# Hybrid attention trunk on one core: eight weight copies spread ahead of the attention, the product with the values' differences two projection steps later, eight projection steps behind the attention

## The chip, the cores and the metric

The kernel runs on one core of a Trainium2 chip. A time is the device time of one execution in microseconds (us). The kernel before took 801.21 us (median of three runs, 800.34 to 802.48). A difference of 0.3%, 2.4 us, is about what a measurement of this kernel can tell from no change.

## What is computed

One layer over 512 tokens of width 2048, all in float32: RMS norm, a sliding-window attention with 32 query heads on 4 key/value heads (window 128, a bucketed relative bias, a sink per head), a gate, an output projection, and then a gated embedding with a second 2048 x 2048 product. Cut to what matters here (the other mixers of the reference are not used at depth 1):

```python
hn = rmsnorm(x, norm_g[0])
q, k, v, gate = split(hn @ w_in)
probs = softmax_with_sink(q @ k.T * 64 ** -0.5 + bias, window 128)
x = x + ((probs @ v) * silu(gate)) @ w_out
emb = p @ ple_proj
x = x + emb * sigmoid(rmsnorm(x, ple_norm) @ ple_gate)
return rmsnorm(x, final_g)
```

## The kernel before

**Arithmetic.** TensorE multiplies numbers that are split into a high and a low part. `mm3` (L123 to L128) issues three matmuls for each product: high by high, low by high, high by low. A weight tile of 128 x 1024 arrives by DMA from SyncE's queue (`wraw`, L102), ScalarE casts the high part (`whi`, L109), VectorE subtracts to get the low part (`wlo`, L110). `wraw`, `whi` and `wlo` have three buffers each.

**Stages.** In the first stage (to about 71 us) the keys, values and first two query tiles are projected. Then thirty further tiles, 14 of q and 16 of the gate (`qps`, `gps`), are projected in 480 steps (16 for a tile, three matmuls each) by the generator `projections`. The first 40 steps (`AHEAD`) run by themselves. The other 440 are dealt out over the attention: the loop over `i` (L906) has 64 blocks of 32 queries and three more turns, and each turn issues the parts of several blocks in a fixed order with six or seven projection steps between them. That order is written out by hand for all engines, so each engine does its instructions as the program issued them.

**A turn of the attention.** Parts of it are generators, and each `next` issues the piece up to the following `yield`. `scores(i)` gives the scores (`s`, L478), bias and minimum on VectorE, the exponential on ScalarE (L522), the reciprocal, and the scaled weights (`pr`, L535). `turn(i - 2)` transposes on TensorE (`pt`, L546), casts on ScalarE (`r`, L557), subtracts on VectorE (L558), then lets GpSimd cut out the triangle (`own`, L565) and ScalarE copy it to the other half (`own`, L574). `weigh(j)` works on a pair of blocks, every second turn: a product of `r` with the values (`o`, L586) and, for the later blocks, a product of `own` with the difference of two value blocks (`o`, L588). A copy on ScalarE (`tmp`, L597) and an addition on VectorE (`u`, L599) then empty the bank. `r` and `own` have one buffer each. The differences are made in the first turns (`make_diff`, L379) and sent to `DV` by SyncE (`spread_diff`, L440).

**Chores.** When a projected tile is done, its three follow-ups go on the list `chores`. For q these are a scaling (L325), a cast (L336) and a subtraction (L334), for the gate L629, L630 and L623. Once the values of a head group are in `u`, `gate_value` (L613) goes on the list `idle`.

**Weight sums.** The output products later use sums of weight blocks. `sum_weights(i)` makes them in DRAM: for even `i` a copy of 512 KB from DRAM to DRAM on SyncE's queue (L692), for odd `i` a DMA of GpSimd that adds another block to a copy made seven steps before (L694). The eight first copies (`SUMS_EARLY` is 16) are issued together, at the end of turn 0.

**After the attention** the remaining chores run, and `unit` multiplies the gated values by `w_out` (`o<-bhi,fho`); its weights are loaded as `braw` (L723) and split as `bhi` and `blo` (L730, L731). In this stage VectorE also makes sums and splits of the gated values (`gate`, `flo`, L835 to L848).

Of the kernel before, what the change touches and what calls it, by code (L numbers as in the profile page):

```python
# [21 lines left out]
KC = D // P  # L22
# [33 lines left out]
def trunk_kernel(ctx: ExitStack, tc: tile.TileContext, a: dict):  # L56
# [25 lines left out]
    def bank(name, tag):  # L82
        return others.get(tag, psum).tile([P, 512], F32, tag=tag, name=name)
# [99 lines left out]
    kinds = [(kind, next(number[kind])) for kind in order]  # L183
# [173 lines left out]
    def make_key(h):  # L357

        t, e = divmod(h, 2)
        k = K[h] = kvq.tile([P, S // QB, 2, QB], F32R, tag="k", name=f"k{h}", bufs=2)  # L360
        same = slice(64 * e, 64 * e + 64)

        def part(low):
            src = kt[t][same].rearrange("p (j k) -> p j k", k=QB)
            for o in (slice(0, 64), slice(64, 128)):
                if low:
                    nc.vector.tensor_sub(k[o, :, 1], src, k[same, :, 0].bitcast(F32))
                else:
                    nc.scalar.copy(k[o, :, 0], src)

        return partial_of(part, False), partial_of(part, True)
# [31 lines left out]
    for b in range(exact, BUCKETS):  # L403
        d = np.nonzero(bk == b)[0]
        if len(d):
            lo, n = P - 1 + int(d.min()), len(d)
# [35 lines left out]
    def first_chores(i, step):  # L442

        if step == 0 and i < NB - 1:
            make_diff(i + 1)
        if step and 1 <= i < NB:
            diffs[i][step - 1]()
        if step == 2 and 1 <= i - 1 < NB:
            spread_diff(i - 1)
        if step and 1 <= i - 2 < NB:  # L450
            split(V[i - 2], values[i - 2])[step - 1]()
# [87 lines left out]
    def turn(i):  # L539


        d, g = divmod(i, UNITS)
        pr = T.pop(i)
        pt = bank(f"pt{i}", "t")[:, :256]
        for u in range(2):
            nc.tensor.transpose(pt[:, u * P : (u + 1) * P], pr[:, u, :], ident)  # L546

        j, part = divmod(i, 2)
        if part == 0:
            own = None  # L550
            if g >= P // TQ:
                own = apool.tile([P, 2, S], F32R, tag="own", name=f"own{j}")
            PT[j] = apool.tile([P, 2, S], F32R, tag="r", name=f"r{j}"), own
        r, own = PT[j]
        rh, rl = (r[:, l].rearrange("p (h t u q) -> p t u h q", h=GROUP, t=2, u=2)[:, part] for l in range(2))
        src = pt.rearrange("p (u h q) -> p u h q", u=2, h=GROUP)
        nc.scalar.copy(rh, src)  # L557
        nc.vector.tensor_sub(rl, src, rh.bitcast(F32))  # L558
        yield
        b = j % 2  # L560
        flat = lambda v, rows: v[rows].rearrange("p l (h t q) -> p t (l h) q", h=GROUP, t=2)[:, part]
        if own is not None:
            rows = slice(0, P) if b else slice(0, HB)
            sign = -1 if b else 1
            nc.gpsimd.affine_select(  # L565
                out=flat(own, rows), in_=flat(r, rows).bitcast(F32), pattern=[[0, 2 * GROUP], [sign, TQ]],
                compare_op=ALU.is_ge, fill=0.0, base=(-HB - 1 if b else 0) + sign * part * TQ, channel_multiplier=-sign,
            )
        yield
        if own is not None:  # L570
            here, there = slice(HB, P), slice(0, HB)
            if not b:
                here, there = there, here
            nc.scalar.copy(flat(own, there)[:, :GROUP], flat(own, here)[:, GROUP:].bitcast(F32))  # L574

    def weigh(j):

        kv, m = divmod(j, S // HB)
        n, b = divmod(m, 2)
        r, own = PT.pop(j)  # L580
        if m == 0:
            U[kv] = apool.tile([P, 4, S], F32, tag="u", name=f"u{kv}", bufs=2)
        out = bank(f"o{j}", "o")
        first = V[0 if n == 0 else n - 1 + b][:, kv]
        for low in range(2):
            nc.tensor.matmul(out, first, r[:, low], start=low == 0, stop=own is None and low == 1)  # L586
        if own is not None:
            nc.tensor.matmul(  # L588
                out, DV[:, n - 1, b, kv * 2 * HD : (kv + 1) * 2 * HD], own[:, 0], start=False, stop=True
            )  # L590
        yield
        ops = out.rearrange("p (u e q) -> p u e q", u=4, e=2)
        dst = U[kv][:, :, m * HB : (m + 1) * HB]
        lower, upper = slice(0, 64), slice(64, 128)
        tmp = [apool.tile([P, 4, HB], F32, tag=f"tmp{e}", name=f"tmp{e}_{j}") for e in range(2)]
        for e, (o, x) in enumerate(((lower, upper), (upper, lower))):
            nc.scalar.copy(tmp[e][o], ops[x, :, e, :])  # L597
        for e, o in enumerate((lower, upper)):
            nc.vector.tensor_add(dst[o], ops[o, :, e, :], tmp[e][o])  # L599
        if m == S // HB - 1:  # L600
            for c in range(4 * kv, 4 * kv + 4):
                weighed.add(c)
                if c in open_gates:
                    idle.append(partial_of(gate_value, c))
# [3 lines left out]
    chores, idle = [], []  # L608
# [78 lines left out]
    SUMS_EARLY = 16  # L687

    def sum_weights(i):

        if i % 2 == 0 and i // 2 < len(copies):
            nc.sync.dma_start(*copies[i // 2])  # L692
        elif i % 2 == 1 and 0 <= i // 2 - 3 < len(adds):
            nc.gpsimd.dma_start(*adds[i // 2 - 3], accum_op=ALU.add, max_dma_last_dim=8192)  # L694
# [181 lines left out]
    def some(of, n=1):  # L876
        for _ in range(min(n, len(of))):
            of.pop(0)()
# [5 lines left out]
    AHEAD = 5 * KC // 2  # L884
    for n in range(AHEAD):
        next(proj)
        if n % 4 == 3 and W.todo:
            W.todo.pop(0)()
        if n > KC and n % 2:
            some(chores)  # L890
    blocks = KVH * UNITS

    def sums_in(i):


        if i == 0:
            return range(0, SUMS_EARLY, 2)
        if i < 4:
            return range(4 * i + 3, min(4 * i + 7, SUMS_EARLY), 2)
        n, of = SUM_STEPS - SUMS_EARLY, blocks - 4  # L900
        return range(SUMS_EARLY + (i - 4) * n // of, SUMS_EARLY + (i - 3) * n // of)

    left = KC * len(kinds) - AHEAD

    softmax = iter(())
    for i in range(blocks + 3):  # L906

        before, softmax = softmax, scores(i) if i < blocks else iter(())
        turned = turn(i - 2) if 2 <= i < blocks + 2 else iter(())
        value = weigh(i // 2 - 2) if 4 <= i and i % 2 == 0 else iter(())  # L910
        next(value, None)
        next(turned, None)
        next(softmax, None)
        next(turned, None)
        next(before, None)
        next(softmax, None)
        first_chores(i, 0)
        if i in (6, 20, 36):
            idle.extend(make_key(1 + i // 16))
        todo = left // (blocks + 2 - i) if i < blocks + 2 else 0  # L920
        left -= todo
        for n in range(max(todo, 6)):
            if n < todo:
                next(proj)
            if n == 0:
                first_chores(i, 1)
                some(W.todo)
                some(chores or idle)
            elif n == 2:
                next(value, None)  # L930
                if len(chores) > 1:
                    some(chores)
            elif n == 3:
                next(turned, None)
                next(softmax, None)
            elif n == 4:
                first_chores(i, 2)
                some(chores or idle)
            elif n == 5:
                next(softmax, None)  # L940
        if i < blocks:
            for n in sums_in(i):
                sum_weights(n)
    for _ in proj:
        pass
    while chores or idle:
        some(chores or idle)
    during.close()
# [429 lines left out]
    n = done[3]  # L1378
# [87 lines left out]
```

## Time and profile before

| what | us |
|---|---|
| median of three runs | 801.21 |
| the profiled execution's own time | 801.74 |
| its span, first to last instruction | 800.0 |
| TensorE busy | 784.2 |
| VectorE busy | 583.8 |
| ScalarE busy | 517.9 |
| GpSimd busy | 150.6 |
| idle time of TensorE that ends on another engine | 6.4 |

The last row adds four lines of the view of waits: 5.0, 0.6, 0.5 and 0.3 us. The profiled execution took 1.74 us more than its span and 0.53 us more than the median. A matmul's duration in the trace is longer than the distance between two starts, since matmuls are pipelined; a busy share of TensorE near 100% therefore says that there is no gap, and the number of matmuls in a stretch says how fast they went. The column PEclk is the share of TensorE's full clock that was granted, the DMA column the busy share of the 16 DMA engines.

### The profile page before, as it was taken

What the parts mean: (1) busy time and instruction counts of PE and PEld (TensorE: products, weight loads), DVE (VectorE), ACT (ScalarE), POOL (GpSimd) and SP (SyncE); (2) the same over time, 40 slices, a digit from 0 to 9 for tenths busy, and PEclk for the clock granted to TensorE, in tenths of its full rate; (3) what the DMA queues carried; (4) which work ended last, traced back from release to release, by engine and by line L of the source; (5) the groups of instructions that cost most, each with busy time, mean ns of one, the idle gap of its engine ahead of it and who ended that gap; (6) DMA issues with size and microseconds to landing.
All of it is one profiled execution on the core that took longest, in us unless ns stands there. A gap on an engine that the chain in (4) does not pass through costs nothing.

```text
span 800.0 us, 11168 instructions
## 1 busy us (share of the span) xinstructions
PE 784.2 (98%) x3658; PEld 650.4 (81%) x3658; DVE 583.8 (73%) x1171; ACT 517.9 (65%) x1131; POOL 150.6 (19%) x252
## 2 busy tenths in 40 slices
PE   9999997999999999999999999999999999999995
PEld 8888885888888888888888887888888888888885
DVE  4538556876876768766776899778877666888896
ACT  6634356877777667766666754457689656756765
POOL 0031121343233413333234200000000020210000
PEclk9999998999999999999999999999999999999998
DMA  9782699999998997989797698767873996796633
GB/s 349 227 245 94 210 241 309 271 261 272 267 262 215 257 257 190 284 209 303 192 267 166 158 353 299 241 207 226 277 264 123 344 197 204 161 232 203 194 105 106
DMA packets 44618, 184.87 MB, mean 231 GB/s; under 512 B 6720, under 2 KB 7232, under 8 KB 39440
## 3 DMA queue, kind: packets, MB, share of 16 engines
q1 hardware_dynamic: 36480, 142.94, 52.0%
q0 software_dynamic: 8080, 41.22, 27.3%
q8 instruction: 29, 0.48, 0.2%
q14 instruction: 29, 0.24, 0.1%
HBM read 177.26 MB, written 62.97 MB: 300 GB/s over the span
## 4 chain that ended last, share of the span: by engine, by line
PE 89%; DVE 3%; DMA 3%; ACT 2%; issue 2%; POOL 0%; SPq 0%; ACTq 0%; DVEq 0%; POOLq 0%
PE gps L126 7%; PE gps L127 7%; PE gps L128 7%; PE qps L126 6%; PE qps L127 6%; PE qps L128 6%; PE g L126 5%; PE g L127 5%; PE g L128 5%; PE o L127 4%; PE o L128 4%; PE o L126 4%; DMA wraw<-in_w_gate_in 2%; PE s L478 2%; PE vps L286 2%; PE o L586 2%
## 5 line engine op out<-in xcount | busy, mean ns | idle before, releaser
L730 ACT CAST bhi<-braw 128x1024 fp32r<-128x1024 f32 x102 | 107.3, 1052 | 74.7 <-PE o L128 21.9
L731 DVE TENSOR_TENSOR blo<-braw,bhi 128x1024 fp32r<-128x1024 f32 x102 | 124.4, 1223 | 40.6 <-ACT bhi L730 40.3
L126 PE MATMUL gps<-xh,whi 128*128 128x512 f32 x256 | 100.4, 392 | 0.0
L127 PE MATMUL gps<-xl,whi 128*128 128x512 f32 x256 | 99.8, 390 | 0.0
L128 PE MATMUL gps<-xh,wlo 128*128 128x512 f32 x256 | 99.7, 389 | 0.0
L110 DVE TENSOR_TENSOR wlo<-wraw,whi 128x1024 fp32r<-128x1024 f32 x60 | 74.0, 1234 | 22.3 <-ACT whi L109 21.3
L126 PE MATMUL qps<-xh,whi 128*128 128x512 f32 x224 | 87.9, 392 | 0.0
L127 PE MATMUL qps<-xl,whi 128*128 128x512 f32 x224 | 87.6, 391 | 0.0
L128 PE MATMUL qps<-xh,wlo 128*128 128x512 f32 x224 | 87.5, 391 | 0.0
L127 PE MATMUL o<-blo,fho 128*128 128x512 f32 x192 | 74.8, 390 | 0.6 <-DVE blo L731 0.6
L126 PE MATMUL g<-bhi,fhg 128*128 128x512 f32 x192 | 75.1, 391 | 0.0
L126 PE MATMUL o<-bhi,fho 128*128 128x512 f32 x192 | 74.8, 390 | 0.0
L128 PE MATMUL o<-bhi,flo 128*128 128x512 f32 x192 | 74.8, 389 | 0.0
L128 PE MATMUL g<-bhi,flg 128*128 128x512 f32 x192 | 74.8, 389 | 0.0
L127 PE MATMUL g<-blo,fhg 128*128 128x512 f32 x192 | 74.7, 389 | 0.0
L109 ACT CAST whi<-wraw 128x1024 fp32r<-128x1024 f32 x60 | 62.3, 1039 | 17.7 <-issue 9.1
L558 DVE TENSOR_TENSOR r<-pt,r 128x256 fp32r<-128x256 f32 x64 | 27.1, 424 | 61.3 <-ACT r L557 60.5
L493 POOL COPY t<-sinkb 128x2 f32<-128x2 f32 x64 | 49.3, 770 | 98.9 <-ACT pr L535 34.3
L565 POOL TENSOR_SCALAR_AFFINE_SELECT own<-r 64x512 fp32r<-64x512 f32 (+1 forms) x48 | 35.4, 737 | 160.0 <-DVE r L558 151.3
L557 ACT CAST r<-pt 128x256 fp32r<-128x256 f32 x64 | 23.7, 370 | 60.6 <-PE pt L546 60.2
L710 POOL DMA_DIRECT2D grown<-in_ple_gate x16 | 13.8, 861 | 232.4 <-DVE blo L731 228.0
L128 PEld LDWEIGHTS gps<-xh,wlo 128*128 128x128 f32 x256 | 48.0, 188 | 10.2
(230 smaller groups left out, 1787.7 us busy)
## 6 DMA issues: line engine op xcount, KB each, us to landing
w_out<-in_w_out POOLq DMA_DIRECT2D x32, 512.0 KB, 8.9
wraw<-in_w_gate_in SPq DMA_DIRECT2D x32, 512.0 KB, 6.6
braw<-w_out SPq DMA_DIRECT2D x32, 512.0 KB, 5.5
wraw<-in_w_q SPq DMA_DIRECT2D x28, 512.0 KB, 6.8
braw<-in_ple_gate SPq DMA_DIRECT2D x24, 512.0 KB, 3.7
braw<-in_w_out SPq DMA_DIRECT2D x22, 512.0 KB, 4.3
xw<-in_first SPq DMA_DIRECT2D x14, 640.5 KB, 6.7
w_out<-in_w_out SPq DMA_DIRECT2D x16, 512.0 KB, 8.9
```

The lines of the kernel that those rows point to most:

```text
L109: nc.scalar.copy(hi, raw)
L110: nc.vector.tensor_sub(lo, raw, hi.bitcast(F32))
L126: nc.tensor.matmul(ps, sh, mh, start=first, stop=False, skip_group_check=more)
L127: nc.tensor.matmul(ps, sh, ml, start=False, stop=False, skip_group_check=more)
L128: nc.tensor.matmul(ps, sl, mh, start=False, stop=last, skip_group_check=more)
L286: nc.tensor.matmul(v_ps[t], h[:, c], part_of(high_at, 256, 512), start=f, stop=e, skip_group_check=True)
L493: nc.gpsimd.tensor_copy(two(0, W + W - 1 if late else W, 1), sinkb[:, d : d + 1].unsqueeze(1).to_broadcast([P, 2, 1]))
L557: nc.scalar.copy(rh, src)
L558: nc.vector.tensor_sub(rl, src, rh.bitcast(F32))
L565: nc.gpsimd.affine_select(out=flat(own, rows), in_=flat(r, rows).bitcast(F32), pattern=[[0, 2 * GROUP], [sign, TQ]], compare_op=ALU.is_ge, ...
L730: nc.scalar.copy(hi, raw)
L731: nc.vector.tensor_sub(lo, raw, hi.bitcast(F32))
```

## The change

Four edits, all to the order in which things are issued; no instruction is added to TensorE, SyncE, GpSimd or ScalarE (3494, 265, 248 and 850 rows on each, before and after).

```diff
@@ weigh
         for low in range(2):
             nc.tensor.matmul(out, first, r[:, low], start=low == 0, stop=own is None and low == 1)
+        yield
         if own is not None:
             nc.tensor.matmul(
                 out, DV[:, n - 1, b, kv * 2 * HD : (kv + 1) * 2 * HD], own[:, 0], start=False, stop=True
@@ the 40 steps ahead of the attention
         if n % 4 == 3 and W.todo:
             W.todo.pop(0)()
-        if n > KC and n % 2:
+        if n >= 2 * KC or n >= KC and n % 2:
             some(chores)
+        if n >= 6 and n % 4 == 2 and n // 4 <= SUMS_EARLY // 2:
+            sum_weights(2 * (n // 4 - 1))
@@ sums_in
         if i == 0:
-            return range(0, SUMS_EARLY, 2)
+            return ()
...
-    left = KC * len(kinds) - AHEAD
+    left = KC * len(kinds) - AHEAD - KC // 2
@@ the attention's turns
                 some(chores or idle)
+            elif n == 1:
+                next(value, None)
             elif n == 2:
-                next(value, None)
                 if len(chores) > 1:
                     some(chores)
             elif n == 3:
                 next(turned, None)
+                next(value, None)
                 next(softmax, None)
@@ behind the attention
     for _ in proj:
-        pass
+        some(chores or idle)
```

**Copies.** The eight first copies are issued one by one in the 40 steps ahead of the attention, after every fourth step from step 6 on. On SyncE's queue, which has no projection steps, they come between the loads of `wraw`. Here `small_0`, `small_1` and `w_out_0_0` to `w_out_1_1` are the eight copies, `bias` the relative bias and `DV` the differences. Before:

```order
L459 DMA bias_839<-tdram 16x144 x8
L102 DMA wraw_885<-in_w_q 128x1024
L102 DMA wraw_917<-in_w_q 128x1024
L102 DMA wraw_955<-in_w_q 128x1024
L102 DMA wraw_991<-in_w_q 128x1024
L102 DMA wraw_1030<-in_w_q 128x1024
L692 DMA small_0_782<-in_w_out 16x8192
L692 DMA small_1_783<-in_w_out 16x8192
L692 DMA w_out_0_0_784<-in_w_out 16x8192
L692 DMA w_out_0_1_785<-in_w_out 16x8192
```

The same place on SyncE after the change:

```order
L459 DMA bias_839<-tdram 16x144 x8
L693 DMA small_0_782<-in_w_out 16x8192
L693 DMA small_1_783<-in_w_out 16x8192
L102 DMA wraw_887<-in_w_q 128x1024
L693 DMA w_out_0_0_784<-in_w_out 16x8192
L693 DMA w_out_0_1_785<-in_w_out 16x8192
L102 DMA wraw_921<-in_w_q 128x1024
L693 DMA w_out_0_2_786<-in_w_out 16x8192
L693 DMA w_out_0_3_787<-in_w_out 16x8192
L102 DMA wraw_961<-in_w_q 128x1024
L693 DMA w_out_1_0_788<-in_w_out 16x8192
L693 DMA w_out_1_1_789<-in_w_out 16x8192
```

Two copies now stand ahead of each of the loads 4, 5, 6 and 7 (`wraw_887`, `wraw_921`, `wraw_961` and the one that follows); before, all eight stood behind load 8. GpSimd's rows are in the same order as before.

**The product with the differences.** In a turn with `weigh`, L588 (L589 after the change) is issued two projection steps after the product with the values. On TensorE in the turn of a later pair, before; `V` are the values, `pt` the transposed weights, `s` the scores:

```order
L586 MATMUL o_1801<-r_1697,V_732 128x512 x2
L588 MATMUL o_1801<-own_1696,DV 128x512
L546 MATMUL pt_1805<-ident,pr_1768 128x128 x2
L478 MATMUL s_1812<-k_735,q_1_709 128x288 x2
L126 MATMUL gps_1715<-xh_563,whi_1664 128x512
```

And after:

```order
L586 MATMUL o_1801<-r_1696,V_732 128x512 x2
L546 MATMUL pt_1804<-ident,pr_1768 128x128 x2
L478 MATMUL s_1811<-k_735,q_1_709 128x288 x2
L126 MATMUL gps_1714<-xh_563,whi_1664 128x512
L127 MATMUL gps_1714<-xl_564,whi_1664 128x512
L128 MATMUL gps_1714<-xh_563,wlo_1665 128x512
L126 MATMUL gps_1714<-xh_594,whi_1664 128x512
L127 MATMUL gps_1714<-xl_595,whi_1664 128x512
L128 MATMUL gps_1714<-xh_594,wlo_1665 128x512
L589 MATMUL o_1801<-own_1695,DV 128x512
```

The transposes, the scores and six projection matmuls have moved ahead of the product with `own`. The copy `tmp` and the addition to `u` now follow the copy to `own` on ScalarE, where they stood ahead of it.

**The last gates.** Eight of the 480 projection steps are kept for after the attention, so a turn has 6.5 steps on average instead of 6.7. At the end of the attention on TensorE, before (`o_0_0` is the first output product):

```order
L127 MATMUL gps_4796<-xl_657,whi_4776 128x512
L128 MATMUL gps_4796<-xh_656,wlo_4777 128x512
L586 MATMUL o_4909<-r_4821,V_733 128x512 x2
L588 MATMUL o_4909<-own_4820,DV 128x512
L126 MATMUL o_0_0_4946<-bhi_4801,fho_00_4829 128x512
```

After:

```order
L128 MATMUL gps_4820<-xh_383,wlo_4747 128x512
L586 MATMUL o_4879<-r_4782,V_733 128x512 x2
L589 MATMUL o_4879<-own_4781,DV 128x512
L126 MATMUL gps_4820<-xh_414,whi_4793 128x512
L127 MATMUL gps_4820<-xl_415,whi_4793 128x512
```

The last pair's products now stand ahead of the last 24 projection matmuls; as many projection matmuls as before (21) stand between the last transposes and those products. Between the eight steps one chore each is issued.

**Chores of the 40 steps.** From step 32 on a chore is issued in every step, not every second one; these are the follow-ups of the second q tile, so its casts and subtractions (L336, L334) come ahead of one weight split.

## The prediction

> **What bounds the kernel now.** I read the page first, then who waits for whom on TensorE, the chain that ended last around the one long wait, and then the queues behind it.
>
> ```profile
> span 800.0 us, 11168 instructions
> PE 784.2 (98%) x3658; PEld 650.4 (81%) x3658; DVE 583.8 (73%) x1171; ACT 517.9 (65%) x1131; POOL 150.6 (19%) x252
> ```
>
> TensorE is the bound; the change gives it no work and takes none. What there is to win are its gaps, and time in which its clock is low. The view of waits gives total, times, longest:
>
> ```profile
> PE o L586 <- ACT r L557: 5.0, 1, 5.0
> ...
> PE o L127 <- DVE blo L731: 0.6, 1, 0.6
> PE o L588 <- ACT own L574: 0.5, 2, 0.3
> PE s L478 <- DVE q L334: 0.3, 1, 0.3
> ```
>
> One wait stands out. The rest of the idle 15.8 us is the start and the tail, which the change does not touch. The stretches with the wait and behind it (TensorE busy and its matmuls; near the end granted clock, DMA share, GB/s):
>
> ```profile
> 120.00:140.00 20.00, 15.04 (x63) 11.54 (x62) 12.64 (x37) 12.76 (x36) 3.70 (x6) 0.83 1.01 309
> 128.00:130.00 2.00, 0.00 (x0) 0.00 (x0) 1.97 (x5) 1.12 (x2) 0.00 (x0) 0.64 1.04 370
> 132.00:134.00 2.00, 2.00 (x7) 1.34 (x7) 1.68 (x8) 1.36 (x7) 0.19 (x1) 0.50 0.92 348
> 140.00:180.00 40.00, 40.00 (x192) 33.26 (x191) 32.49 (x93) 32.02 (x96) 16.36 (x24) 1.00 0.99 266
> ```
>
> Undisturbed, 192 matmuls take 40 us, 0.208 us each. In 120 to 140 only 63 ran, worth 13.1 us. So the wait cost 20 - 13.1 = 6.9 us: 5.0 idle, the other 1.9 after it at a clock of 0.50. The chain says why ScalarE was late with `r`:
>
> ```profile
> 108.53 17.37 DMA wraw<-in_w_gate_in
> 125.92 1.05 ACT whi L109
> ...
> 130.97 0.38 ACT r L557
> 131.39 1.57 PE o L586 x2
> ```
>
> A weight load took 17.4 us, ScalarE stood at its cast, and `r` was behind that cast in ScalarE's fixed order. TensorE did not lack the weight; it lacked `r`.
>
> **Part one, the copies.** SyncE's queue and the DMA engines before that load:
>
> ```profile
> 66.69 1.75 SPq L102 DMA_DIRECT2D wraw<-in_w_q  x2
> ...
> 81.58 3.07 SPq L102 DMA_DIRECT2D wraw<-in_w_q  x2
> ...
> 90.14 1.23 SPq L692 DMA_DIRECT2D small<-in_w_out  x2
> 91.41 3.96 SPq L692 DMA_DIRECT2D w_out<-in_w_out  x6
> 97.42 0.34 SPq L102 DMA_DIRECT2D wraw<-in_w_q  x1
> ```
>
> ```profile
> 66.00:72.00 6.00, 6.00 (x31) 5.02 (x30) 4.04 (x10) 2.84 (x8) 0.00 (x0) 1.00 0.55 184
> 72.00:82.00 10.00, 10.00 (x46) 8.28 (x45) 8.64 (x16) 2.72 (x6) 4.38 (x10) 1.00 0.00 0
> 82.00:90.00 8.00, 8.00 (x37) 6.64 (x36) 4.67 (x7) 3.26 (x6) 0.14 (x1) 1.00 0.41 131
> 90.00:98.00 8.00, 8.00 (x37) 6.64 (x36) 2.50 (x4) 2.32 (x5) 0.85 (x1) 1.00 0.91 315
> 98.00:126.00 28.00, 27.68 (x131) 22.70 (x131) 13.84 (x50) 14.07 (x39) 6.20 (x14) 1.00 1.01 253
> ```
>
> All eight copies go out at 90 to 95 us, and the DMA engines stay full to 126; from 72 to 82 they do nothing. SyncE runs ahead of the program: with nothing to wait for, six copies will go out from 66.7 on, two ahead of load 4, two ahead of load 5 and two behind it, and the last two behind load 6, which waits for its buffer until 81.6. Their price:
>
> ```profile
> q1 hardware_dynamic: 36480, 142.94, 52.0%
> q0 software_dynamic: 8080, 41.22, 27.3%
> ```
>
> SyncE's queue: 52.0% of 800 us for 142.94 MB, 2.9 us for a MB; eight copies of 0.524 MB are 12.2 us of full DMA. GpSimd's: 5.3 us for a MB. Its first two adds follow the first two copies (one queue slot each on GpSimd, order unchanged), so 1.05 MB or 5.6 us move forward too. At most 7.3 us of the copies (0.91 x 8) had passed by 98, so at least 4.9 + 5.6 = 10.5 of the 28 saturated us go: a share near 0.6. In the early stretch 12.2 + 5.6 us meet 10 us of empty engines, half of 66 to 72 and half of 82 to 90; they fit.
>
> How soon must the load of 108.5 then land? ScalarE's rows:
>
> ```profile
> 117.02 1.05 ACT L109 CAST whi<-wraw 128x1024 fp32r<-128x1024 f32 x1 [2.36 <-DMA wraw<-in_w_q]
> ...
> 125.92 1.05 ACT L109 CAST whi<-wraw 128x1024 fp32r<-128x1024 f32 x1 [4.82 <-DMA wraw<-in_w_gate_in]
> ```
>
> Without both DMA waits (7.2 us) `r` ends near 124.2 instead of 131.35; TensorE comes to its product near 126.4. So there are 2.2 us in hand, the cast may start as late as 125.92 - 7.18 + 2.2 = 120.9, and the load may take 12.4 us. All landings of weight loads from 60 to 200 us:
>
> ```profile
> DMA to landing us min/median/max: 3.6/7.4/19.6
> ```
>
> The bounds are 3.6 and 19.6 us; I take the median 7.4, measured mostly with the engines full. The wait goes whole, and the low clock with it: **6.9 us**. If that cover goes (a load of 15 us), 2.6 us of waiting come back. SyncE pays 5.2 us of issue time, now ahead of loads 4 to 7; load 4 goes out 1.2 us later, load 5 some 2.5. By the median load 4 lands near 76.
>
> [...]
>
> **Part two, the product with the differences.** The two waits for `own` are 0.5 us. One of them:
>
> ```profile
> 234.19 0.63 PE L586 MATMUL o<-r,V 128*128 128x512 f32 x2
> 235.12 0.51 PE L588 MATMUL o<-own,DV 128*128 128x512 f32 x1 [0.30 <-ACT own L574]
> ```
>
> Six matmuls, transposes and scores now stand ahead of it, over 1.3 us, against a shortage of at most 0.3. Both waits go. Each short wait also drew out the next matmul, 0.51 or 0.50 us against 0.39 (the row for `blo` below), so 0.1 more each: **0.7 us**. In the last turn no step lies between the two products, but 21 projection matmuls still cover `own` as before: nothing.
>
> **Part three, the chores.** The q subtraction comes ahead of one weight split of 1.2 us, against a wait of 0.3; it goes: **0.4 us**. The split that now stands behind it is popped at step 35 and its weights are first used at step 48, 13 steps or 39 x 0.208 = 8 us on: nothing.
>
> **Part four, the last gates.** Behind the attention VectorE is full:
>
> ```profile
> 454.00:484.00 30.00, 29.70 (x131) 24.04 (x129) 29.02 (x36) 15.90 (x23) 3.25 (x3) 1.00 0.76 280
> 484.29 0.50 PE L127 MATMUL o<-blo,fho 128*128 128x512 f32 x1 [0.58 <-DVE blo L731]
> L127 PE MATMUL o<-blo,fho 128*128 128x512 f32 x192 | 74.8, 390 | 0.6 <-DVE blo L731 0.6
> ```
>
> VectorE is busy for 29.0 of 30 us there, and the wait at its end is 0.6 us. The change lets the last sums and three gate values run while TensorE has 24 projection matmuls (24 x 0.208 = 5.0 us). A shift of 0.7 us is enough, so the wait goes: **0.7 us**. From below: VectorE's work is not less, and if the new order puts gate work ahead of a `blo`, the wait stays or grows by one such instruction (+0.6). I take the gain, since work that was behind 454 now lies ahead of it.
>
> **The sum**: 6.9 + 0.7 + 0.4 + 0.7 = 8.7 us. Ends of projected tiles now fall at other places in the turns, which gave the waits of 0.3; I allow two new ones, 0.6 us. That leaves 8.1: 801.74 - 8.1 = 793.6 for the profiled execution, which lies 0.5 above its median of 801.21. So 793.1.
>
> **Rivals.**
>
> *Part of the wait stays.* The load at 108.5 still meets GpSimd's adds, the pieces of `DV` and the next copies. Against it: a share near 0.6. For it: two of those loads landed in 17 to 20 us here. Above 12.4 us each us costs one; at 15 to 16 us, 2.6 to 3.6 come back: 796 to 797.
>
> *The change doesn't do what it says: the stall moves to the front.* Loads 4 to 7 stand behind copies in one queue.
>
> ```profile
> 98.76 0.38 PE L478 MATMUL s<-k,q 128*128 128x32 f32 x2 [0.32 <-DVE q L334]
> ```
>
> Load 4 is needed by the eight steps that end at 98.4, so 24 x 8.00/37 = 5.2 us before, at 93.2, and cast and subtraction take 2.3. From 67.9 that leaves 23 us, beyond the longest 19.6. If it fails, one long wait replaces another: 800. [...]
>
> *Slower: one buffer of `own`.* The select (L565) for the next pair must wait until L588 has read `own`, and L588 is now later; behind the select stand GpSimd's adds and the sink copies, behind ScalarE's copy of `own` now `tmp` and the exponential. There are 24 such products. Each may be late by the whole move of 1.5 us: 36 us at worst, nothing at best. It outweighs the gain from 8.7/24 = 0.36 us each; at 0.47 the time is 803.8. Against it:
>
> ```profile
> ACT own L574 <- POOL own L565: 4.6, 4, 3.1
> ...
> 236.97 0.71 POOL L565 TENSOR_SCALAR_AFFINE_SELECT own<-r 64x512 fp32r<-64x512 f32 x1 [4.23 <-DVE r L558]
> ```
>
> In that turn the select came 2.8 us after L586 started, later than the moved product will end (234.19 + 0.5 + 0.5 + 1.3 + 0.2 = 236.7). ScalarE waited for a select four times in all.
>
> **How the numbers follow.** The forecast has 0.68, with its own range 792 to 795 (all waits gone and none new: 792.5; four or five new ones of 0.3 and a load of 13 us: 795). Part of the wait 0.16, the moved stall 0.07, slower 0.06, and 0.03 for more gain than I count. The range 791.5 to 797.0 holds the forecast and most of the first rival, 0.8. About 0.3% (2.4 us) is what a measurement here can tell: faster 0.68 + 0.16 + 0.03 = 0.87, same 0.07, slower 0.06.
>
> **What would show it.** Right: no wait of L586 for `r` near 126; clock 1.00 from 120 to 140, with 94 to 96 matmuls there; the DMA share in 72 to 82 well above 0; the load at 108 landing in under 12 us; no wait for `own`. Wrong: a wait for `whi` or `wlo` of loads 4 to 7 before 110; a first output product that waits for `flo` or `blo`; ScalarE's waits for GpSimd's `own` in many turns.

## The result, and the profile after

The changed kernel takes 797.47 us (median of 4 runs, 797.15 to 797.64); the kernel before, run beside it, takes 801.61 (4 runs, 800.34 to 802.48). The ratio is 0.9949, with a 95% interval of 0.9932 to 0.9966. The change gains 4.1 us, half of the 8.1 forecast, and the time lies 0.5 us beyond the upper end of the range. The profiled execution took 797.58 us, 795.9 of it span.

The view of TensorE's waits after (total, times, longest; only the wait at the start of the program is left out):

```profile
PE o L586 <- DVE r L558: 1.8, 3, 1.0
PE s L478 <- DVE sm L511: 1.5, 4, 0.4
```

All four waits that the prediction listed are gone: `r` of ScalarE (5.0), `blo` (0.6), `own` (0.5) and `q` (0.3). In their place stand two kinds that the kernel before did not have, 3.3 us together: the product with the values waits for `r` of VectorE, and the scores wait for VectorE's reading of the scores before (L511).

The stretches of the first part, after (span, TensorE busy and its matmuls, then weight loads, VectorE, ScalarE, GpSimd, clock, DMA share, GB/s):

```profile
72.00:82.00 10.00, 10.00 (x45) 8.26 (x44) 8.48 (x16) 2.91 (x6) 4.57 (x11) 1.00 0.85 306
...
98.00:126.00 28.00, 27.93 (x133) 22.83 (x131) 17.33 (x54) 18.00 (x48) 5.40 (x13) 1.00 0.83 214
120.00:140.00 20.00, 18.61 (x88) 14.95 (x87) 15.21 (x39) 15.09 (x44) 4.38 (x7) 1.00 0.95 282
140.00:180.00 40.00, 39.37 (x187) 32.14 (x186) 32.11 (x95) 31.02 (x95) 15.28 (x25) 1.00 1.01 274
```

From 72 to 82 the DMA engines now work at 0.85 where they had stood at 0.00. The granted clock is 1.00 all through 120 to 140 (it was 0.83). But 88 matmuls ran there, not the forecast's 94 to 96, and in 140 to 180 there are 187 where before there were 192: something takes time that took none before.

SyncE's queue and the chain behind the load that had been late:

```profile
66.44 2.32 SPq L693 DMA_DIRECT2D small<-in_w_out  x2
...
71.22 1.12 SPq L693 DMA_DIRECT2D w_out<-in_w_out  x2
...
81.76 1.12 SPq L693 DMA_DIRECT2D w_out<-in_w_out  x2
```

```profile
107.84 10.75 DMA wraw<-in_w_gate_in
...
120.92 0.62 DVE qps L325
...
121.57 0.58 ACT q L336
```

Six copies go out between 66.4 and 72.3 and the last two at 81.8, as forecast. The load took 10.75 us instead of 17.37, under the 12.4 that the prediction allowed. The chain does not end there, though: it goes on through a split, a scaling (L325) and ScalarE's cast of a q tile (L336). What stands behind that cast is where the rest of the gain went, as the experiments below show.

Four times, TensorE's own rows look like this. The timeline of TensorE after, from the product with the values (L586) to the next projection matmul, at the four places:

```profile
125.53 0.40 PE L586 MATMUL o<-r,V 128*128 128x512 f32 x1
126.94 0.50 PE L586 MATMUL o<-r,V 128*128 128x512 f32 x1 [1.01 <-DVE r L558]
...
128.44 0.39 PE L126 MATMUL qps<-xh,whi 128*128 128x512 f32 x1
...
166.79 0.40 PE L586 MATMUL o<-r,V 128*128 128x512 f32 x1
...
168.95 0.40 PE L126 MATMUL gps<-xh,whi 128*128 128x512 f32 x1
...
207.17 0.81 PE L586 MATMUL o<-r,V 128*128 128x512 f32 x2
...
208.63 0.50 PE L478 MATMUL s<-k,q 128*128 128x288 f32 x2 [0.37 <-DVE sm L511]
208.97 0.39 PE L126 MATMUL gps<-xh,whi 128*128 128x512 f32 x1
...
247.33 0.40 PE L586 MATMUL o<-r,V 128*128 128x512 f32 x1
...
249.73 0.39 PE L126 MATMUL qps<-xh,whi 128*128 128x512 f32 x1
```

From the first product to the next projection matmul it takes 2.91, 2.16, 1.80 and 2.40 us.

Why `r` is late is read from ScalarE and VectorE at the second of these places. ScalarE after:

```profile
162.22 1.17 ACT L336 CAST q<-qps 64x512 fp32r<-64x512 f32 x2 [2.36 <-DVE qps L325]
...
163.71 0.74 ACT L598 COPY tmp<-o 64x256 f32<-64x256 f32 x2
```

VectorE after:

```profile
164.48 0.86 DVE L600 TENSOR_TENSOR u<-o,tmp 64x256 f32<-64x256 f32 x2 [2.30 <-ACT tmp L598]
165.35 1.39 DVE L334 TENSOR_TENSOR q<-qps,q 64x512 fp32r<-64x512 f32 x2
...
166.97 0.42 DVE L558 TENSOR_TENSOR r<-pt,r 128x256 fp32r<-128x256 f32 x1
```

ScalarE comes to its cast of `q` 2.36 us too early and stands there. Behind the cast stands `tmp`, the copy that takes the finished product from its PSUM bank. VectorE needs `tmp` for the addition to `u`, and stands 2.30 us in its turn; behind that addition stand the q subtraction, the reciprocal, and the low part of `r` for which TensorE waits. The same kind of turn in the kernel before, ScalarE and VectorE:

```profile
166.33 0.75 ACT L597 COPY tmp<-o 64x256 f32<-64x256 f32 x2
168.21 1.17 ACT L336 CAST q<-qps 64x512 fp32r<-64x512 f32 x2 [1.13 <-DVE qps L325]
```

```profile
168.08 0.85 DVE L599 TENSOR_TENSOR u<-o,tmp 64x256 f32<-64x256 f32 x2
169.41 1.39 DVE L334 TENSOR_TENSOR q<-qps,q 64x512 fp32r<-64x512 f32 x2 [0.48 <-ACT q L336]
...
171.14 0.42 DVE L558 TENSOR_TENSOR r<-pt,r 128x256 fp32r<-128x256 f32 x1
```

TensorE in that turn:

```profile
172.88 0.63 PE L586 MATMUL o<-r,V 128*128 128x512 f32 x2
```

There `tmp` stood ahead of the cast. ScalarE copied while it would have waited anyway, VectorE added at once, and `r` was done at 171.56, 1.3 us ahead of TensorE. (Ends are starts plus durations: 171.14 + 0.42.)

A fifth turn of the changed kernel has the same order, and TensorE does not wait there. VectorE and TensorE in it:

```profile
323.22 0.86 DVE L600 TENSOR_TENSOR u<-o,tmp 64x256 f32<-64x256 f32 x2 [2.30 <-ACT tmp L598]
```

```profile
326.83 0.63 PE L586 MATMUL o<-r,V 128*128 128x512 f32 x2
```

VectorE stands for `tmp` as long as at the second place, and `r` is done at 326.13, 0.7 us ahead of TensorE. The difference is the cover: between the transposes and the product this turn has seven projection steps (21 matmuls, 5.2 us), and the four others have six (18 matmuls, 4.6 us). In the kernel before, the turns with six steps end with the product at 211.98; with eight steps kept for the end they go on to the one at 247.33. So the fourth place lies in a turn that another part of the change, the last gates, had shortened. No run shows what it would have cost without that.

### The profile page after: what moved, and what is told of

Read it like the earlier page. It is cut to its first block, busy times and chain, and to the rows that moved or that the text cites. A ratio compares the mean times of both kernels' runs of the same rounds, so it can differ in the third digit from the quotient of the medians.

```text
span 795.9 us, 11177 instructions
## 1 busy us (share of the span) xinstructions
PE 783.1 (98%) x3658; PEld 649.4 (82%) x3658; DVE 590.7 (74%) x1171; ACT 517.4 (65%) x1131; POOL 141.7 (18%) x252
## 4 chain that ended last, share of the span: by engine, by line
PE 92%; DVE 4%; ACT 2%; DMA 1%; issue 1%; SPq 0%; ACTq 0%; DVEq 0%
PE gps L126 7%; PE gps L127 7%; PE gps L128 7%; PE qps L126 6%; PE qps L127 6%; PE qps L128 6%; PE g L128 5%; PE o L128 5%; PE g L127 5%; PE o L127 5%; PE o L126 5%; PE g L126 5%; PE vps L286 2%; PE s L478 2%; PE o L586 2%; PE pt L546 1%
## 5 line engine op out<-in xcount | busy, mean ns | idle before, releaser
L493 POOL COPY t<-sinkb 128x2 f32<-128x2 f32 x64 | 41.3, 646 | 108.6 <-ACT pr L535 39.4
L126 PEld LDWEIGHTS gps<-xh,whi 128*128 128x128 f32 x256 | 48.1, 188 | 8.9
L127 PEld LDWEIGHTS gps<-xl,whi 128*128 128x128 f32 x256 | 48.1, 188 | 8.7
```

Of the source, the lines that this page charges most:

```text
L126: nc.tensor.matmul(ps, sh, mh, start=first, stop=False, skip_group_check=more)
L127: nc.tensor.matmul(ps, sh, ml, start=False, stop=False, skip_group_check=more)
L493: nc.gpsimd.tensor_copy(two(0, W + W - 1 if late else W, 1), sinkb[:, d : d + 1].unsqueeze(1).to_broadcast([P, 2, 1]))
```

## The experiments

**The theories.** The second part of the change moves two things: the product with the differences, from right behind the product with the values to two projection steps later (slot 1 of the turn), and the emptying of that bank (`tmp`, `u`) from slot 2 to slot 3. In slot 2 one chore is issued, so the emptying moved from ahead of that chore to behind it. *The first theory (T1)* is that this alone made the waits at the four places, since in those turns that chore is the cast of a q tile. *The second (T2)* is that the product with the differences is itself too late. *The third (T3)* is that the early copies delay weight loads elsewhere, so that casts come late in ScalarE's order. The times of before, run beside the kernels below, are 800.91 us for the first four and 801.44 for the others.

**The emptying put back** ahead of slot 2's chore, all else as in the change:

```diff
             elif n == 2:
+                next(value, None)
                 if len(chores) > 1:
                     some(chores)
             elif n == 3:
                 next(turned, None)
-                next(value, None)
                 next(softmax, None)
```

> The changed kernel with one thing undone: the bank of weigh is emptied in the third of the six slots of a turn again (n == 2), ahead of the q casts, and not in the fourth (n == 3) behind them; the product with the differences stays two projection steps late. Theory 1, the late evacuation (ScalarE's copy tmp stands behind q casts that wait for VectorE, and VectorE's addition to u waits for tmp, with the q subtraction, the reciprocal and the low part of r behind it, at the four turns in which a q tile ends): all four pairs of waits of TensorE (o for r, s for sm) go, 3.3 us of idle time and about 0.1 us for each restart, 797.5 - 4.1 = 793.4 us. Theory 2, the late product with the differences (one buffer of own, GpSimd's select behind it): the product stays where it is, so 797.5 us. Theory 3, the copies remove less than the stall: 797.5 us, with the wait near 127 still there.

It takes 792.01 us (5 runs, 791.87 to 793.95), ratio 0.9887 (0.9872 to 0.9902). Its view of TensorE's waits, TensorE's rows at the first of the four places, and VectorE's there:

```profile
PE warm_ps L141 <- PEq L1461: 0.9, 1, 0.9
```

```profile
125.42 0.63 PE L586 MATMUL o<-r,V 128*128 128x512 f32 x2
...
126.37 0.39 PE L126 MATMUL qps<-xh,whi 128*128 128x512 f32 x1
```

```profile
121.45 0.85 DVE L600 TENSOR_TENSOR u<-o,tmp 64x256 f32<-64x256 f32 x2
...
124.40 0.42 DVE L558 TENSOR_TENSOR r<-pt,r 128x256 fp32r<-128x256 f32 x1
```

No wait is left behind the start. From the first product to the next projection matmul it is now 126.37 - 125.42 = 0.95 us, and the same at the three other places; this prices the four places: 2.91 + 2.16 + 1.80 + 2.40 - 4 x 0.95 = 5.5 us. The two medians differ by 797.47 - 792.01 = 5.5, the two ratios by 5.0. So the four places account for the whole difference. Counting matmuls from 120 to 320 gives the same; the windows of the change and of this kernel:

```profile
120.00:320.00 200.00, 196.73 (x925) 161.13 (x924) 154.17 (x434) 145.96 (x430) 64.69 (x113) 1.00 0.94 258
```

```profile
120.00:320.00 200.00, 200.00 (x952) 165.86 (x951) 158.97 (x447) 151.00 (x445) 67.27 (x116) 1.00 0.95 266
```

27 matmuls more, at 0.208 us each 5.6 us. The product with the differences and the copies stand here exactly as in the change, so neither of the other two theories can explain the four places. This version beats both kernels.

**The copies alone** in the kernel before:

```diff
+        if n >= 6 and n % 4 == 2 and n // 4 <= SUMS_EARLY // 2:
+            sum_weights(2 * (n // 4 - 1))
...
         if i == 0:
-            return range(0, SUMS_EARLY, 2)
+            return ()
```

> The kernel before with only the eight copies moved ahead of the attention. Theories 1 and 2: the stall near 126 goes whole, 6.9 us, and nothing is given back, since the evacuation and the product are where they were: 801.6 - 6.9 = 794.7 us, with the waits of 0.3 and 0.6 us still there. Theory 3, the copies remove less than the stall: 797 to 798 us, with a wait of over 1 us near 127.

794.31 us (4 runs, 794.0 to 794.76), ratio 0.9909 (0.9896 to 0.9923): the copies alone are worth 6.6 us by the medians and 7.3 by the ratio, about the forecast's 6.9. The longest group of TensorE's waits is now:

```profile
PE o L588 <- ACT own L574: 1.0, 3, 0.5
```

Besides it stand the old ones for `blo` and `q`. The wait for `r` is gone and the waits for `own` are 0.5 us longer in all, no more: the copies do not make later loads cost anything near 4 us. The third theory falls. One part of the change alone is faster than the whole.

**The emptying moved alone**, in the kernel before, the product staying where it was:

```diff
             elif n == 2:
-                next(value, None)
                 if len(chores) > 1:
                     some(chores)
             elif n == 3:
                 next(turned, None)
+                next(value, None)
                 next(softmax, None)
```

> The kernel before with only the evacuation moved from the third slot to the fourth (n == 2 to n == 3); the product with the differences stays right behind the one with the values, the copies together. Theory 1: slower, the turns in which a q tile ends make TensorE wait, three of them for 0.6 to 0.9 us with restarts of 0.2, and the stall near 126 is longer by up to 1 us: 801.6 + 3 = 804.6 us (803.5 to 806). Theories 2 and 3: no change, 801.6 us.

805.89 us (5 runs, 805.55 to 806.6), ratio 1.0055 (1.0042 to 1.0068): slower by 4.4 us by the ratio, 5.0 by the medians. TensorE's waits:

```profile
PE o L586 <- ACT r L557: 4.6, 1, 4.6
PE o L586 <- DVE r L558: 1.9, 2, 1.7
...
PE s L478 <- DVE sm L511: 0.4, 1, 0.4
```

The waits for VectorE's `r` and for L511 appear in a kernel that has nothing else of the change; those for `own` (line left out) grow from 0.5 to 1.3. Two lines of code that only move an emptying cost two thirds of what the copies gain.

**The product with the differences moved alone**, the emptying staying ahead of the chore:

```diff
             nc.tensor.matmul(out, first, r[:, low], start=low == 0, stop=own is None and low == 1)
+        yield
         if own is not None:
...
+            elif n == 1:
+                next(value, None)
             elif n == 2:
                 next(value, None)
```

> The kernel before with only the product with the differences moved two projection steps later; the evacuation stays in the third slot (n == 2). Theories 1 and 3: the two waits for own go, 0.5 to 0.7 us, and nothing new comes: 801.0 us. Theory 2: the selects behind the late product make r or own late, 803 to 806 us.

800.56 us (11 runs, 799.98 to 801.31), ratio 0.9989 (0.998 to 0.9998): a gain of 0.9 us where the forecast's term was 0.7 (0.2 to 1.6 by the interval, 0.35 by the medians). The second theory falls. The waits for `own` are gone, and the one for `blo` as well, which the forecast had put down to another part. What is left of TensorE's waits is the long one, now 4.6, beside the 0.3 of the scores for `q`.

**Order or lateness?** In the change the emptying is both behind the chore and a slot later. Two kernels tell these apart. The first, from the version with the emptying put back, keeps it in slot 2 but issues it behind the chore:

```diff
             elif n == 2:
-                next(value, None)
                 if len(chores) > 1:
                     some(chores)
+                next(value, None)
             elif n == 3:
```

> The kernel with the evacuation back in the third slot (n == 2), but behind the chore of that slot and not ahead of it. Theory 1 as an order: the waits come back, 797 us (796 to 798), with VectorE's addition to u waiting about 2 us for tmp at four turns. Theory 1 as a matter of the late slot: 792 us, no waits.

796.97 us (6 runs, 796.48 to 799.5), ratio 0.9951 (0.9937 to 0.9964): within half a microsecond of the change. TensorE's waits are of the kinds and the size of the change's:

```profile
PE o L586 <- DVE r L558: 1.7, 2, 1.5
PE s L478 <- DVE sm L511: 1.5, 4, 0.4
```

One thing in this trace the change's does not have. Behind the first place, where a wait of 1.47 us and one of 0.37 follow each other, the granted clock is 0.51 for three microseconds:

```profile
129.00:132.00 3.00, 3.00 (x8) 2.42 (x9) 2.16 (x10) 2.89 (x9) 1.22 (x3) 0.51 0.67 253
```

The traced execution took 799.5 us, the others 796.5 to 797.6 at a higher mean clock (0.996 or 0.997, against 0.994). So the order brings the waits back, and what they cost seems to vary from one execution to the next; only one execution was traced.

The second kernel is the change with the emptying in slot 3 and slot 2's chore issued behind it:

```diff
-            elif n == 2:
-                if len(chores) > 1:
-                    some(chores)
             elif n == 3:
                 next(turned, None)
                 next(value, None)
+                if len(chores) > 1:
+                    some(chores)
                 next(softmax, None)
```

> The changed kernel with the evacuation left in the fourth slot (n == 3), but the chore of the third slot (a q cast in the turns where a q tile ends) issued behind it, still ahead of the exponential. Theory 1 as an order of instructions (the copy tmp behind a q cast that waits): the four pairs of waits go, 792 to 793 us, as with the evacuation in the third slot. Theory 1 as a matter of the late slot itself (the bank is emptied a slot later, whatever stands ahead): 797 us, the waits stay.

795.46 us (5 runs, 794.77 to 795.78), ratio 0.9928 (0.9915 to 0.9941). This lies between what the two sides expected. TensorE's waits, and VectorE ahead of one of them:

```profile
PE s L478 <- DVE sm L511: 0.7, 2, 0.4
PE s L478 <- DVE q L334: 0.7, 2, 0.4
```

```profile
137.57 1.39 DVE L334 TENSOR_TENSOR q<-qps,q 64x512 fp32r<-64x512 f32 x2
138.89 1.38 DVE L367 TENSOR_TENSOR k<-kt,k 64x512 fp32r<-64x512 f32 x2
140.30 0.17 DVE L524 RECIPROCAL sm<-sm 128x2 f32<-128x2 f32 x1
```

No product waits for `r` any more, so the order is what made those waits. But the chore was moved too: subtractions of `q` and of `k` now stand in one row ahead of a reciprocal, and the scores wait. My expectation missed that a chore moved by a slot is not free either. What these waits cost can be measured over all turns together. The first of the products with the values that come after 115 us starts at 115.76 in the version with the emptying put back and at 115.78 here; the 24th, in that version and here:

```profile
354.86 0.63 PE L586 MATMUL o<-r,V 128*128 128x512 f32 x2
```

```profile
357.71 0.63 PE L586 MATMUL o<-r,V 128*128 128x512 f32 x2
```

Between them lie 239.10 and 241.93 us, 2.8 us more here, and all of it falls in the turns of the four waits (1.6 us around the first two, 0.5 and 0.7 around the others). The two profiled executions, 791.90 and 794.77, differ by 2.9. So the moved chore explains the distance to the version with the emptying put back in the traces; by the medians that distance is 3.4.

**The other two parts alone**, each in the kernel before. The last gates:

```diff
-    left = KC * len(kinds) - AHEAD
+    left = KC * len(kinds) - AHEAD - KC // 2
...
     for _ in proj:
-        pass
+        some(chores or idle)
```

> The kernel before with only the eight projection steps kept for after the attention. The working of the prediction: the wait of 0.6 us for blo near 484 goes, 0.7 us, and nothing else changes: 800.3 us against 801.0. Rival: the ends of the tiles fall in other turns and the wait goes for that reason or comes elsewhere, 800 to 802 us, with other small waits of 0.3 to 0.5 us.

799.74 us (11 runs, 799.14 to 801.03), ratio 0.9982 (0.9974 to 0.9991): a gain of 1.4 us. The wait for `blo` is gone, and so are the two for `own`, probably since with fewer projection steps in a turn the ends of tiles fall in other turns. That `blo` is not waited for does not show that the last gates did it: the wait is missing as well from the traces of the emptying alone, the product alone and the chores alone, which leave the last gates as they were. And the chores of the 40 steps:

```diff
-        if n > KC and n % 2:
+        if n >= 2 * KC or n >= KC and n % 2:
             some(chores)
```

> The kernel before with only the denser chores in the 40 steps ahead of the attention. The working of the prediction: the wait of s for q (0.3 us at about 98.7) goes, 0.4 us: 800.6 us against 801.0. Rival: the split that moves behind the q subtraction makes something later wait, no change.

801.5 us (11 runs, 799.66 to 801.98), ratio 1.0001 (0.9992 to 1.001): nothing. In its trace the wait of the scores for `q` is gone, and one of 0.42 for L511 stands in a later turn, at 121.78.

## Why the prediction was wrong, point by point

- **What bounds the kernel, and the long wait: right.** The 6.9 us for the stall and the low clock behind it measured 6.6 to 7.3. Each link held: the copies go out in the empty stretch, the load lands in 10.75 us, ScalarE stands 0.59 us at its cast instead of 4.82, the clock stays at 1.00. The margin was smaller than worked out: in the version with the emptying put back `r` is done at 124.82 and TensorE arrives at 125.42, 0.6 us in hand where I had 2.2 (124.2 and 126.4). The share of DMA from 98 to 126 fell from 1.01 to 0.83, not to 0.6. Nor did the copies quite fit ahead: 17.8 us of transfers against 10 + 0.45 x 6 + 0.59 x 8 = 17.4 us of free engines, and the share from 82 to 90 after is 0.96.
- **The product with the differences: right in itself** (0.7 forecast, 0.9 measured alone). The waits for `own` went. That the sizes agree is partly luck, since the wait for `blo` (0.6) is missing from that trace too.
- **The last gates and the chores: the sum of the two was near** (1.1 forecast, 1.4 and 0 measured). The split between them was not: the chores only shifted a wait. The reason given for the last gates is not shown either, since the wait for `blo` also goes in kernels without that edit. The 1.4 us are near the listed waits that went: `blo` 0.6, `own` 0.5, and 0.2 of the long one.
- **The failed step** is in part two, and one term of the sum shows its size: "Ends of projected tiles now fall at other places in the turns, which gave the waits of 0.3; I allow two new ones, 0.6 us." New waits did come, but they cost 5.5 us, nine times the allowance. I costed the product's move and put that of the emptying, which the same edit carries past a chore, at nothing without a reason. I had seen that `tmp` now follows the copy to `own` on ScalarE, and did not ask what else had come ahead of it. Without that term the sum was 8.7 us; with the emptying put back the gain is 9.05 us by the ratio, 8.9 by the medians. So the sum of the terms came out, in part by luck as the two points above say, and the allowance did not.
- **It could be worked out from the rows of before.** There the cast of `q` ends at 168.21 + 1.17 = 169.38. With `tmp` behind it (0.75), the addition to `u` would start near 170.1 instead of 168.08, end near 171.0, and the subtraction of `q` would start there instead of at 169.41: 1.6 us later, and `r` with it. In hand were 1.3 us. A shortfall of some 0.3 us for the product, and the scores behind it: a pair of short waits in each turn where `tmp` stands behind such a cast. The cover of six projection steps belongs to that working: four of the five such turns after the change have it and wait, the fifth has seven and does not.
- **The rivals.** *Part of the wait stays* named a time near the one measured (796 to 797), but not the mechanism: the load was not late (10.75 us). *The stall moves to the front* did not happen; no cast or split of loads 4 to 7 holds TensorE. *One buffer of `own`*: half of it is true. From GpSimd's view of waits after:

```profile
POOL own L565 <- PE o L589: 55.1, 15, 5.9
```

The select does wait for the late product, fifteen times. But no wait of TensorE hangs on it: the version with the emptying put back has the late product as well, and TensorE waits for nothing. That rival even named `tmp` as standing behind ScalarE's copy of `own`, but the harm came from the cast of `q` ahead of it, and on VectorE.

- **The size of a short wait.** I priced one at its length plus 0.1. The view lists 3.3 us at the four places, and they cost 5.5: at 207.17 the only listed stop is 0.37, yet the sequence is 1.80 - 0.95 = 0.85 longer. The pair L586 took 0.81 there against 0.63: part of the stop is drawn as busy time. In the changed kernel's trace the granted clock stays at 1.00 through waits of up to 1.01 us (the first place, 125 to 133), so the extra there is not the clock. In the trace with the emptying behind the chore in slot 2 the clock does fall, to 0.51 from 129 to 132, behind waits of 1.47 and 0.37 us; before, it stood at 0.50 from 132 to 134, behind the wait of 5.0 us. What makes it fall after one wait and not after another these runs do not show. My price had nothing for a lower clock and only 0.1 us for what a stop draws out, and was too low in both ways.

## What to carry to other kernels

When a step is moved, list everything it is moved past on each engine, and for each of those ask what it waits for: here `tmp`, put behind a cast that waited 2.36 us, kept VectorE standing 2.30 us at the addition, with the q subtraction, the reciprocal and `r` behind it. Compare that delay with what the consumer has in hand in the very turns where the slow neighbour occurs, and after every change of how much work lies in a turn. And price a stop of the busiest engine by a whole sequence, from its first instruction to the next undisturbed one, against the same sequence elsewhere, since the listed idle time was 3.3 of 5.5 us here.

## What was not expected of the hardware

Weight loads from 60 to 200 us after, from issue to landing:

```profile
DMA to landing us min/median/max: 3.7/9.2/13.8
```

The median rose from 7.4 to 9.2 us while the longest fell from 19.6 to 13.8. With the copies spread over the loads the usual load lands later and the worst one earlier. TensorE waits for none of them now: before, the one that held it was among the longest (17.37), and a median of 9.2 us stays below the 12.4 that the place of that load allowed.
